# Warming products of 64 columns with none behind the last, and MLP weight roundings in halves in six of eight phases

## The chip, the core and the metric

The kernel runs on one core of a Trainium2 chip. The metric is the device time of one execution in microseconds (us); less is better. A second time, the span, is read from a profiled execution: it goes from the program's first to its last instruction.

## The reference

One transformer block on 512 rows of width 1024, in float32. A gated linear attention and a latent attention are merged, projected and added to the input `h`; then comes the MLP that the change touches:

```python
m = rmsnorm(h, g_mlp[l])
h = h + jnp.square(jax.nn.relu(m @ w_ff1[l])) @ w_ff2[l]
return rmsnorm(h, g_final)
```

`w_ff1` is 1024 x 4096, `w_ff2` 4096 x 1024. The first product of the whole program is a projection of the normed input on columns of `w_in`.

## The kernel before, in words

**Precision.** Each float32 operand is split in two fp32r tiles: a rounded part, whose name ends in `h` (ScalarE, ACT, rounds it by `activation(..., AF.Copy)`), and the remainder, whose name ends in `l` (VectorE, DVE, subtracts the rounded part from the source). A product is three matmuls on TensorE (PE): high by high, high by low, low by high (`mm3`, line 128).

**Start.** The first operands come by DMA. While they travel, PE multiplies a constant by itself into a bank that nobody reads (`warm`, lines 370 to 373): seven products of 128 columns and one of 64. In the profile each of these float32 products stands as two PE instructions, two passes, so `warm x16` is eight products. After them come the products called `first` (`first_by_sides`, line 450), in pieces of 256 columns, as the ACT and DVE roundings of their operands get done. This part is held in program order on each engine (`in_program_order(fixed)`, line 540).

**MLP.** The hidden width is done in four quarters (`NQ = 4`). Each quarter has two phases, `f` (`m @ w_ff1`) and `g` (the squared result `@ w_ff2`); the eight phases are `Mlp(0)` to `Mlp(7)`, called f0, g0, f1, g1, f2, g2, f3, g3, and `self.n` is the number. Each phase forms its 2 x 2 block product by seven block products (a scheme of the Strassen kind), called m = 1 to 7. For each m the weights stand in two groups `g` of 128 x 1024 elements; `hi(m, g)` (line 1725) rounds one into a tile such as `g031h` (phase g0, m = 3, group 1) and `lo(m, g)` (line 1737) makes the remainder `g031l` on DVE. A group is two pieces `p` of 128 x 512, which PE takes one after the other: in an f phase as the stationary operand, in a g phase as the moving one. The rounded tiles have four buffers of each kind (`halves`, line 251), so a rounding waits until PE has done with the product two before. In phases 2 and 4 (f1 and f2) a rounding is two ACT instructions of 128 x 512; in the other six it is one of 128 x 1024.

ACT does other work in between: copies of the f results out of their banks, relu, square, and the rounding of the squared rows (`left_hi`). DVE makes the remainders, adds the g results to the rows `h` (`add_rows`) and forms sums of blocks. Which step stands where is written by hand: tables of times (`PLACES`, `F0_PLACES`) sort the steps, and the order so made is kept on every engine (`in_program_order(written)`, line 2181).

**End.** `last_rows` (line 1878) finishes the last block product, norms the rows and stores them. The last product that counts goes into the bank `gend`. Behind it stand twelve products of 64 columns of `ones_r` into a bank `tail` (lines 1912 to 1914), which nobody reads. The order of the last steps is the string `LAST_ROWS` (`P:` is PE, `A:` ACT, `D:` DVE, `G:` GpSimd, `S:` the DMA queue of SyncE).

Of the kernel before, what the change touches and what calls it, by code (L numbers as in the profile page):

```python
# [18 lines left out]
P = 128  # L19
S = 512  # L20
NT = S // P
D = 1024
# [75 lines left out]
def tile_block(ctx: ExitStack, tc: tile.TileContext, t, out: bass.AP):  # L98
    nc = Held(tc.nc)
# [9 lines left out]
    def u2(name, dt=F32, shape=(P, S)):  # L109
        return tl(list(shape), dt, "u2", 29, name)  # L110

    def u4(name, dt=F32R, shape=(P, 2, S)):
        return tl(list(shape), dt, "u4", 26, name)
# [4 lines left out]
    def ps(tag, name):  # L118
        serial[0] += 1
        return pp.tile([P, S], F32, tag=tag, bufs=4, name=f"{name}_{serial[0]}")  # L120

    def one(shape, dt, name):
        return sb.tile(shape, dt, tag=name, bufs=1, name=name)
# [9 lines left out]
    def split(hi, lo, src, rest=nc.vector):  # L133
        nc.scalar.activation(hi, src, AF.Copy)
        rest.tensor_tensor(lo, src, raw(hi), op=ALU.subtract)
# [48 lines left out]
    ones_r = one([P, P], F32R, "ones_r")  # L184
# [66 lines left out]
    def halves(nk, nw, name):  # L251
        wh = tl([P, nk, nw], F32R, "wh", 4, f"{name}h")
        wl = tl([P, nk, nw], F32R, "wl", 4, f"{name}l")
        return wh, wl
# [114 lines left out]
    fixed = traced()  # L369
    warm = ps("at", "warm")  # L370
    heat = nc.const_aps.tensor(1.0, [P, P])
    for n in [P] * 7 + [P // 2]:
        nc.tensor.matmul(warm[:, :n], heat, heat[:, :n], start=True, stop=True)
    f_accs = [ps("mm", f"first{i}") for i in range(NT)]
    vh = [halves(2, S, f"first{k}") for k in range(KD // 2)]
    sq = None
# [1200 lines left out]
    def add_rows(i, c, acc, op=ALU.add):  # L1577
        hc = hrow[i][:, c * S : (c + 1) * S]
        nc.vector.tensor_tensor(hc, hc, acc, op=op)
# [115 lines left out]
    class Mlp:  # L1695
# [29 lines left out]
        def hi(self, m, g):  # L1725
            if (self.n, m) == (0, 1):
                self.right[m, g] = [u4(f"{self.name}{m}{g}{x}") for x in "hl"]
            else:
                self.right[m, g] = halves(2, S, f"{self.name}{m}{g}")
            src, to = self.tile_of(m)[g], self.right[m, g][0]  # L1730
            if self.n in (2, 4):
                for p in range(2):
                    nc.scalar.activation(to[:, p], src[:, p], AF.Copy)
            else:
                nc.scalar.activation(to, src, AF.Copy)
# [95 lines left out]
    def out_begin(i):  # L1831
        if not spare:
            spare.append(u2("junk"))
            nc.scalar.activation(ones_r, ident, AF.Copy)
            nc.scalar.activation(spare[0][:, 0:1], ident[:, 0:1], AF.Sqrt)
        hparts[i] = sm(f"hp{i}", 6)
        ms_rows[i] = u4(f"ms{i}", F32, (P, D))

    def out_square(i, src, n, at=0):
        nc.scalar.activation(  # L1840
            spare[0][:, at : at + src.shape[1]], src, AF.Square, accum_out=hparts[i][:, n : n + 1]
        )

    def out_mean(i):
        p = hparts[i]
        nc.gpsimd.tensor_scalar(p[:, 2:3], p[:, 0:1], 1.0 / D, EPS, op0=ALU.mult, op1=ALU.add)

    def out_added(i, n):
        p = hparts[i]
        nc.vector.scalar_tensor_tensor(  # L1850
            p[:, 2:3], p[:, n : n + 1], 1.0 / D, p[:, 2:3], op0=ALU.mult, op1=ALU.add
        )

    def out_rstd(i, n=1):
        p = hparts[i]
        nc.scalar.activation(p[:, 3:4], p[:, n : n + 1], AF.Sqrt, bias=p[:, 2:3], scale=1.0 / D)
        nc.vector.reciprocal(p[:, 5:6], p[:, 3:4])

    def out_gained(i, cols, eng=nc.gpsimd, src=None):
        src = hrow[i][:, cols] if src is None else src  # L1860
        eng.tensor_tensor(ms_rows[i][:, cols], src, gains[0][:, cols], op=ALU.mult)

    def out_scaled(i, cols, by_vector=False):
        o, rs = ms_rows[i][:, cols], hparts[i][:, 5:6]
        if by_vector:
            nc.vector.tensor_scalar(o, o, rs, None, op0=ALU.mult)
        else:
            nc.scalar.activation(o, o, AF.Copy, scale=rs)

    def out_left(i):  # L1870
        nc.vector.scalar_tensor_tensor(
            ms_rows[i][:, LEFT], hrow[i][:, LEFT], hparts[i][:, 5:6], gains[0][:, LEFT], op0=ALU.mult, op1=ALU.mult
        )

    def out_store(i, a, b, queue=nc.sync):
        queue.dma_start(out[0, i * P : (i + 1) * P, a:b], ms_rows[i][:, a:b])

    def last_rows(ph):

        accs, end = ph.acc_of[7], ps("mm", "gend")[:, 0:HT]  # L1880
        rest = u2("hend", F32R, (P, 2, HT))
        for i in (2, 3):
            out_begin(i)
            out_square(i, hrow[i][:, RIGHT], 0)
            out_mean(i)
            out_gained(i, RIGHT)
        split(rest[:, 0], rest[:, 1], hrow[3][:, QUARTERS[1]])
        nc.scalar.activation(end, accs[1][:, QUARTERS[1]], AF.Copy)
        for p in range(NP):
            ph.second_product(4, accs[0], False, 0, p)  # L1890
        for i in range(2):
            out_scaled(i, RIGHT)
            for a in (S, S + HT):
                out_store(i, a, a + HT)
            out_left(i)
            for a in (0, HT)[: 2 - i]:
                out_store(i, a, a + (HT, S)[i])
        add_rows(2, 0, accs[0])
        out_square(2, hrow[2][:, LEFT], 1)
        last = accs[1][:, QUARTERS[0]]  # L1900
        for p in range(NP):
            ph.second_product(4, last, False, 1, p, QUARTERS[0])
        out_rstd(2)
        nc.vector.tensor_tensor(hrow[3][:, QUARTERS[0]], last, hrow[3][:, QUARTERS[0]], op=ALU.add)
        out_square(3, hrow[3][:, QUARTERS[0]], 1)
        out_gained(3, QUARTERS[0], nc.vector)
        for p in range(NP):
            ph.second_product(4, end, False, 1, p, QUARTERS[1])
            if p == 2:
                for x in range(2):  # L1910
                    nc.tensor.matmul(end, ones_r, rest[:, x], start=False, stop=False, skip_group_check=True)
        tail = ps("mm", "tail")
        for _ in range(12):
            nc.tensor.matmul(tail[:, : P // 2], ones_r, ones_r[:, : P // 2], start=True, stop=True)
        out_scaled(2, RIGHT)
        out_store(2, S, D)
        out_left(2)
        out_store(2, 0, S)
        out_added(3, 1)
        out_square(3, end, 4, HT)  # L1920
        out_gained(3, QUARTERS[1], nc.vector, end)
        out_rstd(3, 4)
        cut = S + HT // 2
        out_scaled(3, slice(0, cut), True)
        out_scaled(3, slice(cut, D))
        out_store(3, 0, cut)
        out_store(3, cut, D, nc.scalar)
# [93 lines left out]
    for x in range(2):  # L2021
# [67 lines left out]
        P:g3x0*3 A:junk D:f3l41 G:hp0 A:hp0 P:g3x0*3 A:junk D:g340l P:g3x0*3 A:junk P:g3x1*3 D:f3l40 G:hp1 D:hp0  # L2089
        P:g3x0*3 A:hp1 A:g341h G:ms1 D:h2 D:hp1 A:ms0 S:out*2 P:g3x1*3 A:junk P:g3x1*3 D:g341l G:hp2 G:ms2 P:g3x1*3 A:gend D:ms0 S:out*2  # L2090
        A:ms1 S:out*2 D:h3 G:ms3 A:junk P:g3x0*12 D:ms1 S:out G:hp3 D:h2 D:hend A:junk
        P:g3x1*12 A:hp2 D:hp2 A:ms2 S:out D:h3 A:junk D:ms2 S:out D:ms3 D:hp3 P:gend*14 P:tail*12 A:junk D:ms3 A:hp3 D:hp3 D:ms3
        A:ms3 S:out A:out
    """
    FIRST, SECOND, PERIOD = 36, 22.77, 7857
# [81 lines left out]
    for _, _, what, args in [x for x in steps if x[0] >= last]:  # L2177
        what(*args)
    last_rows(g3)
    nc.emit(LAST_ROWS)  # L2180
    in_program_order(written)


def build(arrays):
    nc = bacc.Bacc("TRN2", target_bir_lowering=False, num_devices=1, dynamic_dma_scratch_size=8192)  # L2185
    t = {
        n: nc.dram_tensor(f"in_{n}", list(a.shape), mybir.dt.from_np(a.dtype), kind="ExternalInput").ap()
        for n, a in arrays.items()
    }
    out = nc.dram_tensor("out_0", [1, S, D], F32, kind="ExternalOutput").ap()  # L2190
    with tile.TileContext(nc) as tc:
        tile_block(tc, t, out)
    return nc
# [21 lines left out]
```

## Time and profile before

| | before |
|---|---|
| time, median of 3 runs | 733.57 us (733.51 to 733.57) |
| time of the profiled execution | 733.74 us |
| its span | 732.0 us |
| PE busy | 726.9 us, 99% of the span |
| DVE busy | 621.4 us, 85% |
| ACT busy | 502.2 us, 69% |
| GpSimd (POOL) busy | 224.6 us, 31% |

A row of the timeline reads: start in us from the span's start, length in us, engine, line, operation, what is written <- what is read, shape, count, and in brackets the engine's idle time ahead of it with what ended it. `PEld` is the loading of weights into PE, which overlaps with its matmuls. Equal instructions that follow each other are one row. Lines 76 and 90 are those of a helper that issues every instruction, so the tiles' names tell the rows apart. Matmul ends are modelled and overlap the next start: the step from start to start is what counts. `L2185` and the like are the program's frame.

### The profile page before, as it was taken

Reading aid. Unit: us, or ns where it says so; the run is one execution under the profiler, and the core shown is the slowest. Engines: PE = TensorE matmul, PEld = TensorE weight load, DVE = VectorE, ACT = ScalarE, POOL = GpSimd, SP = SyncE. Lnnn points to the kernel's source line nnn. Section 1 sums busy time; section 2 is a strip of 40 time slices with the busy share of each in tenths; the row PEclk is TensorE's granted clock in tenths of the full one; section 3 lists DMA queues with packets and bytes.
Section 4 is the critical chain, followed back from the end, with each engine's and each line's share of the span. In section 5 each row is a group of like instructions: output and inputs, shape, how many; then the busy total and the mean of one; then the engine's idle time right before and its main releaser. Section 6 shows DMA issues by size and latency. Waiting matters only on the chain.

```text
span 732.0 us, 11458 instructions
## 1 busy us (share of the span) xinstructions
PE 726.9 (99%) x4174; PEld 641.4 (88%) x4174; DVE 621.4 (85%) x861; ACT 502.2 (69%) x853; POOL 224.6 (31%) x283
## 2 busy tenths in 40 slices
PE   9999999999999999999999999999999999999997
PEld 8888888888898888888888999889988998899986
DVE  7777788889988887789989789998699869987797
ACT  7657565595686864988867889545774477546966
POOL 0742020234843843225873512200111012100224
PEclk9999999999999999999999999999999999999999
DMA  9848693431222334657957899871988078815754
GB/s 303 287 130 197 198 193 94 72 58 45 58 59 59 73 62 96 194 157 187 242 102 194 205 201 203 188 218 54 244 181 205 9 225 202 205 59 138 179 90 142
DMA packets 81625, 109.96 MB, mean 150 GB/s; under 512 B 16256, under 2 KB 35584, under 8 KB 81568
## 3 DMA queue, kind: packets, MB, share of 16 engines
q1 hardware_dynamic: 64192, 75.71, 33.3%
q0 software_dynamic: 17088, 33.30, 27.2%
q8 instruction: 33, 0.54, 0.3%
q10 hardware_dynamic: 288, 0.22, 0.1%
q14 instruction: 24, 0.20, 0.1%
HBM read 104.22 MB, written 2.10 MB: 145 GB/s over the span
## 4 chain that ended last, share of the span: by engine, by line
PE 97%; ACT 1%; POOL 1%; issue 1%; DVE 0%; POOLq 0%; ACTq 0%
PE first L90 3%; PE f3x L90 3%; PE f2x L90 3%; PE f1x L90 3%; PE f0x L90 3%; PE s L76 3%; PE av L76 3%; PE wox L76 3%; PE g2x L90 3%; PE g1x L90 3%; PE g0x L90 3%; PE gvx L90 3%; PE zax L90 3%; PE grx L90 3%; PE gk L90 2%; PE cq L90 2%
## 5 line engine op out<-in xcount | busy, mean ns | idle before, releaser
L90 POOL DMA_DIRECT2D w<-in_w_ff x32 | 38.6, 1205 | 240.1 <-DMA w<-in_w_ff 129.3
L76 ACT ACTIVATE e<-s,top 128x512 f32<-128x512 f32 x32 | 21.9, 687 | 8.1 <-DVE top L76 7.1
L76 PE MATMUL s<-kbuf,q 96*128 96x512 f32 x96 | 26.6, 403 | 0.0
L76 DVE TENSOR_REDUCE top<-s 128x1 f32<-128x512 f32 x32 | 21.6, 684 | 5.7 <-PE s L76 5.4
L76 PE MATMUL av<-pT,v 128*128 128x512 f32 (+1 forms) x108 | 25.4, 372 | 0.0
L76 DVE TENSOR_TENSOR pT<-tp,pT 128x512 fp32r<-128x512 f32 x32 | 21.7, 685 | 2.2 <-PE s L76 0.9
L76 ACT ACTIVATE pT<-tp 128x512 fp32r<-128x512 f32 x32 | 18.6, 600 | 5.8 <-PE tp L76 5.5
L76 PEld LDWEIGHTS av<-pT,v 128*128 128x128 f32 x108 | 18.6, 189 | 3.3
L76 PEld LDWEIGHTS s<-kbuf,q 96*128 96x128 f32 x96 | 17.0, 189 | 3.1 <-DVE grb L76 0.2
L76 PE MATMUL tp<-ident,e 128*128 128x128 f32 x128 | 17.9, 272 | 0.0
L76 PEld LDWEIGHTS tp<-ident,e 128*128 128x128 f32 x128 | 15.2, 140 | 2.7 <-ACT e L76 0.3
L90 POOL DMA_DIRECT2D gvw<-in_w_in x4 | 4.8, 1226 | 38.7 <-DVE gvw L90 34.0
L90 POOL TENSOR_TENSOR qF<-qk,qF 128x512 fp32r<-128x512 f32 x3 | 5.3, 1757 | 32.8 <-ACT qF L90 32.8
L90 POOL DMA_DIRECT2D zaw<-in_w_in x4 | 4.8, 1218 | 33.0 <-DVE zaw L90 28.3
L76 POOL DMA_DIRECT2D w<-in_w_ff x8 | 10.0, 1358 | 15.1 <-DVE g360l L76 7.1
L90 DVE TENSOR_TENSOR w<-w,w 128x1024 f32<-128x1024 f32 x12 | 14.4, 1222 | 0.1
L90 ACT ACT_TABLE_LOAD x9 | 11.5, 1283 | 1.2 <-PEq L2185 0.8
L76 POOL DMA_DIRECT2D w<-in_w_out x10 | 12.2, 1445 | 0.0
L76 POOL TENSOR_TENSOR my<-tb,yg 128x256 f32<-128x256 f32 x8 | 7.2, 899 | 13.7 <-DVE tb L76 7.5
L76 ACT ACTIVATE e<-e,tot 128x512 f32<-128x512 f32 x16 | 11.3, 721 | 0.0
L90 ACT ACTIVATE f1h<-f1a 128x512 fp32r<-128x512 f32 x10 | 6.1, 623 | 6.2 <-DVE f1a L90 6.2
L90 ACT ACTIVATE f0h<-f0a 128x512 fp32r<-128x512 f32 x10 | 6.1, 623 | 6.2 <-DVE f0a L90 6.2
(1979 smaller groups left out, 3106.0 us busy)
## 6 DMA issues: line engine op xcount, KB each, us to landing
w<-in_w_ff SPq DMA_DIRECT2D x48, 512.0 KB, 5.9
w<-in_w_ff POOLq DMA_DIRECT2D x40, 512.0 KB, 6.3
w<-in_w_out POOLq DMA_DIRECT2D x10, 512.0 KB, 6.1
grw<-in_w_in SPq DMA_DIRECT2D x8, 512.0 KB, 9.9
zaw<-in_w_in SPq DMA_DIRECT2D x8, 512.0 KB, 6.2
gvw<-in_w_in SPq DMA_DIRECT2D x8, 512.0 KB, 4.5
w<-in_w_out SPq DMA_DIRECT2D x16, 256.0 KB, 4.2
w221f<-in_w_ff SPq DMA_DIRECT2D x8, 512.0 KB, 5.0
```

The lines of the kernel that those rows point to most:

```text
L76: what(*args, **options)
L90: return what(*args, **options)
```

## The change

It has three edits.

1. The warming products become fifteen of 64 columns: 960 columns, as before (7 x 128 + 64), in 30 passes where there were 16.
2. The twelve `tail` products, and their bank, go.
3. `hi` rounds in two halves of 128 x 512 in all phases but f0 and g3: f1 and f2 did so already; g0, g1, g2 and f3 are new. That is 4 phases x 14 roundings = 56 more ACT instructions.

```diff
-    for n in [P] * 7 + [P // 2]:
-        nc.tensor.matmul(warm[:, :n], heat, heat[:, :n], start=True, stop=True)
+    for _ in range(15):
+        nc.tensor.matmul(warm[:, : P // 2], heat, heat[:, : P // 2], start=True, stop=True)
...
             src, to = self.tile_of(m)[g], self.right[m, g][0]
-            if self.n in (2, 4):
+            if 0 < self.n < 7:
                 for p in range(2):
                     nc.scalar.activation(to[:, p], src[:, p], AF.Copy)
             else:
...
-        tail = ps("mm", "tail")
-        for _ in range(12):
-            nc.tensor.matmul(tail[:, : P // 2], ones_r, ones_r[:, : P // 2], start=True, stop=True)
...
-P:gend*14 P:tail*12 A:junk
+P:gend*14 A:junk
```

No instruction of another kind moves: on DVE, GpSimd and SyncE the rows stand as before. The numbers in the names below are serials, which the added instructions shift.

PE's first rows before; `warm` is the bank that nobody reads, `first` are the accumulators of the first projection:

```order
L90 MATMUL warm_121<-const-float32-1.0 128x128 x7
L90 MATMUL warm_121<-const-float32-1.0 128x64
L90 MATMUL first_25_130<-xT_1_82,first0h_134 128x256
L90 MATMUL first_26_131<-xT_1_82,first0h_134 128x256
L90 MATMUL first_25_130<-xT_1_82,first0l_135 128x256
```

The same place now:

```order
L90 MATMUL warm_121<-const-float32-1.0 128x64 x15
L90 MATMUL first_25_137<-xT_1_82,first0h_141 128x256
L90 MATMUL first_26_138<-xT_1_82,first0h_141 128x256
L90 MATMUL first_25_137<-xT_1_82,first0l_142 128x256
L90 MATMUL first_26_138<-xT_1_82,first0l_142 128x256
```

Only the shape and the count of the warming rows differ; the first product keeps its place behind them.

ACT at the opening of phase g0 before; `g020h` to `g051h` are weight roundings, `f0a` relu and square of the rows of f0, `f0h` their roundings, `f0s` sums of blocks:

```order
L90 ACTIVATE g020h_4990<-w_30_802_2855 128x1024
L90 ACTIVATE f0a_977_4756<-f0a_977_4756 128x512
L90 ACTIVATE g021h_5009<-w_31_803_2856 128x1024
L90 ACTIVATE f0a_978_4757<-f0a_978_4757 128x512
L90 ACTIVATE f0h_1013_5021<-f0a_977_4756 128x512
L90 ACTIVATE f0a_978_4757<-f0a_978_4757 128x512
L90 ACTIVATE f0h_1014_5022<-f0a_978_4757 128x512
L90 ACTIVATE f0a_970_4686<-f0a_970_4686 128x512
L90 ACTIVATE f0h_1017_5042<-f0s_1001_4968 128x512
L90 ACTIVATE g050h_5051<-w_20_734_2787 128x1024
```

The same place now:

```order
L90 ACTIVATE g020h_4999<-w_30_802_2862 128x512 x2
L90 ACTIVATE f0a_977_4763<-f0a_977_4763 128x512
L90 ACTIVATE g021h_5019<-w_31_803_2863 128x512 x2
L90 ACTIVATE f0a_978_4764<-f0a_978_4764 128x512
L90 ACTIVATE f0h_1013_5032<-f0a_977_4763 128x512
L90 ACTIVATE f0a_978_4764<-f0a_978_4764 128x512
L90 ACTIVATE f0h_1014_5033<-f0a_978_4764 128x512
L90 ACTIVATE f0a_970_4693<-f0a_970_4693 128x512
L90 ACTIVATE f0h_1017_5053<-f0s_1001_4977 128x512
L90 ACTIVATE g050h_5062<-w_20_734_2794 128x512 x2
```

Each rounding is two rows' worth in the place of one; what stands between them stays where it was.

PE's last rows before; `gend` is the bank of the last product, `g341h` and `g341l` the last weights, `f3h` and `f3l` the squared rows, `hend` a part of the rows that is added on PE:

```order
L76 MATMUL gend_7526<-hend_7527,ones_r 128x256 x2
L76 MATMUL gend_7526<-g341h_7519,f3h_1322_7336 128x256
L76 MATMUL gend_7526<-g341l_7520,f3h_1322_7336 128x256
L76 MATMUL gend_7526<-g341h_7519,f3l_1324_7338 128x256
L76 MATMUL tail_7532<-ones_r 128x64 x12
L2191 UNCONDITIONAL_BRANCH
```

The same place now:

```order
L76 MATMUL gend_7589<-hend_7590,ones_r 128x256 x2
L76 MATMUL gend_7589<-g341h_7582,f3h_1322_7399 128x256
L76 MATMUL gend_7589<-g341l_7583,f3h_1322_7399 128x256
L76 MATMUL gend_7589<-g341h_7582,f3l_1324_7401 128x256
L2188 UNCONDITIONAL_BRANCH
```

The `tail` row is gone, and nothing takes its place.

More of the change, by code (lines that the diff above doesn't have):

```diff
@@ L2091, in tile_block @@
         A:ms1 S:out*2 D:h3 G:ms3 A:junk P:g3x0*12 D:ms1 S:out G:hp3 D:h2 D:hend A:junk
-        P:g3x1*12 A:hp2 D:hp2 A:ms2 S:out D:h3 A:junk D:ms2 S:out D:ms3 D:hp3 P:gend*14 P:tail*12 A:junk D:ms3 A:hp3 D:hp3 D:ms3
+        P:g3x1*12 A:hp2 D:hp2 A:ms2 S:out D:h3 A:junk D:ms2 S:out D:ms3 D:hp3 P:gend*14 A:junk D:ms3 A:hp3 D:hp3 D:ms3
         A:ms3 S:out A:out
```

## Prediction

> **What bounds the kernel now.** I read the page first, for the share of each engine and the chain that ended last:
>
> ```profile
> span 732.0 us, 11458 instructions
> ...
> PE 726.9 (99%) x4174; PEld 641.4 (88%) x4174; DVE 621.4 (85%) x861; ACT 502.2 (69%) x853; POOL 224.6 (31%) x283
> ...
> PE 97%; ACT 1%; POOL 1%; issue 1%; DVE 0%; POOLq 0%; ACTq 0%
> ```
>
> PE is busy for 726.9 of 732.0 us and is 97% of the chain. A busy PE may still step slowly, so next I asked the waits of PE alone. The whole answer is one row, the wait for the program's start:
>
> ```profile
> PE warm L90 <- PEq L2185: 0.8, 1, 0.8
> ```
>
> Then the busy times by stage: the phases f1, f2, f3 (the first three rows), g1 and g2. Columns: from:to, length, then busy time and count of PE, PEld, DVE, ACT, POOL, the granted clock, the DMA share and rate.
>
> ```profile
> 490.81:531.13 40.32, 40.32 (x338) 40.32 (x337) 31.01 (x32) 26.23 (x46) 3.73 (x4) 1.00 0.51 137
> 569.23:609.55 40.32, 40.32 (x338) 40.32 (x337) 31.01 (x32) 26.25 (x46) 3.76 (x4) 1.00 0.51 137
> 647.65:687.97 40.32, 40.32 (x338) 40.32 (x337) 31.04 (x32) 25.25 (x35) 3.73 (x4) 1.00 0.46 112
> 531.13:569.23 38.10, 38.10 (x170) 31.54 (x170) 36.46 (x48) 22.67 (x33) 5.90 (x5) 1.00 0.81 187
> 609.55:647.65 38.10, 38.10 (x170) 31.53 (x170) 36.45 (x48) 22.50 (x30) 5.90 (x5) 1.00 0.79 187
> ```
>
> An f phase has 336 products of 256 columns (the other two of the 338 began before), so a step is 40.32 / 336 = 0.120 us, and it is the same in all three. PE runs at its own pace through the MLP: nothing that makes weights ready earlier can shorten it, only something that makes them late can lengthen it. What is left to move lies before the first full-speed product and behind the last one.
>
> **Edit 1, the warming.** The start, by the timeline of PE, and then the rows of the `warm` and `tail` tiles' passes (count, shortest, median and longest in ns; nobody waits for `tail`), the timeline's row of `tail`, ACT's first rounding and a stage of PE alone (from:to, length, busy, count, clock, DMA):
>
> ```profile
> 0.84 3.65 PE L90 MATMUL warm<-const-float32-1.0 128*128 128x128 f32 x16 [0.84 <-PEq L2185]
> ...
> 3.75 0.53 PE L90 MATMUL warm<-const-float32-1.0 128*128 128x128 f32 x2
> ...
> 3.75 0.74 PE L90 MATMUL warm<-const-float32-1.0 128*128 128x128 f32 x3
> 4.28 0.80 PE L90 MATMUL first<-xT,first0h 128*128 128x256 f32 x2
> 4.87 0.63 PE L90 MATMUL first<-xT,first0l 128*128 128x256 f32 x2
> ...
> 6.15 0.71 PE L90 MATMUL first<-xT,first0h 128*128 128x256 f32 x3
> ```
>
> ```profile
> L90 PE MATMUL warm<-const-float32-1.0 x16: 314/421/550, 0.8 to 4.1; 128*128 128x128 f32 x14, 128*128 128x64 f32 x2
> ...
> L76 PE MATMUL tail<-ones_r x12: 194/277/277, 726.3 to 727.4; 128*128 128x64 f32 x12
> ...
> who waited for it (us, times):
> ...
> 726.29 1.42 PE L76 MATMUL tail<-ones_r 128*128 128x64 f32 x12
> ...
> 3.71 0.51 ACT L90 ACTIVATE xT<-xw 128x256 fp32r<-128x256 f32 x1 [1.63 <-DMA xw<-in_first]
> ...
> 6.58:8.98 2.40, 2.40 (x22) 1.00 1.04 380
> ```
>
> First, two speeds. From 4.87 to 6.15 stand six `first` products (three rows of two), (6.15 - 4.87) / 6 = 0.213 us each; from 6.58 to 8.98 stand 20 of the same shape (22 less the two that began before), 0.120 us each. The clock opens at 6.58. A us by which the real products start later is work done at the slow step, so it costs 1 - 0.120 / 0.213 = 0.44 us at the end.
>
> Second, how long the new warming takes. Before it, 13 passes of 128 columns lie between 0.84 and 3.75: 0.224 each, which includes the start of the first. The two short passes: the row of two ends at 3.75 + 0.53 = 4.28 with the pass of 0.314, which so began at 3.97; the row of three ends at 4.49 with one of 0.421, which so began at 4.07. So a pass of 64 columns, with a full load of 128 x 128 weights of its own, took about 0.10 to 0.11 us at the slow clock, half of a long one. Bounds for a pass of 64: 0.104 from below (the rows of `tail`, 12 passes at the fast clock: (1.42 - 0.277) / 11, where 0.277 is the length of one), and 0.213 from above (as if the columns made no difference). I take 0.112, half of 0.224, since the one direct row lies there. Then 30 passes take 3.36 us where the old 16 ended at 4.07 + 0.11 = 4.18, or 3.34 after 0.84. With a start-up of 0.14 on top (13 x (0.224 - 0.213)) the new ones end between 4.20 and 4.34. The first product waits for ACT's rounding anyway, 3.71 + 0.51 = 4.22, and began at 4.28; an end at 4.34 would make that 4.35, so all but 0.07 is hidden. On the path: 0 to 0.07 x 0.44 = 0.03 us. I take 0.03. If the cover were gone too, 0.07.
>
> [...]
>
> **Edit 2, the tail.** The end, from the last product that counts:
>
> ```profile
> 726.17 0.28 PE L76 MATMUL gend<-g341h,f3l 128*128 128x256 f32 x1
> ...
> 726.79 0.36 ACT L76 ACTIVATE junk<-gend 128x256 f32<-128x256 f32 x1
> ...
> 727.86 0.62 ACT L76 ACTIVATE ms<-ms,hp 128x384 f32<-128x384 f32 x1 [0.29 <-DVE hp L76]
> 728.51 0.36 ACTq L76 DMA_DIRECT2D out<-ms  x1
> ```
>
> PE's `tail` ends at 726.29 + 1.42 = 727.71; ACT goes on to 728.48, its store is issued at 728.51, and the span lasts to 732.0. Nobody waits for `tail`, and it stands behind everything that counts, so its 1.42 us are off the path: 0. The bounds are 0 both ways but for what follows on ACT and DVE being slower or faster without PE at work beside them, of which these rows show nothing.
>
> **Edit 3, the halves.** What two halves cost against one whole, in the same step of f1 and of f3 (ACT's timeline):
>
> ```profile
> 485.38 1.16 ACT L90 ACTIVATE f110h<-w 128x512 fp32r<-128x512 f32 x2 [0.93 <-PE g0x L90]
> ...
> 640.89 1.06 ACT L90 ACTIVATE f310h<-w 128x1024 fp32r<-128x1024 f32 x1
> ```
>
> 1.16 against 1.06: 0.10 us more, 56 x 0.10 = 5.6 us of ACT in four phases, 1.4 us in each. ACT is idle for 40.32 - 25.25 = 15 us in f3 and 38.10 - 22.67 = 15 us in g1. The halves free the first half for PE some 0.4 us earlier, which is worth nothing, since PE waits for none. For f3 the answer stands in the table above: f1 and f2 are that very code with halves, and take the same 40.32 us. In the g phases no row shows halves, so I looked for the tightest place, g0's m = 3, which recurs in g1 and g2:
>
> ```profile
> 453.39 1.05 ACT L90 ACTIVATE g021h<-w 128x1024 fp32r<-128x1024 f32 x1
> ...
> 464.68 0.63 ACT L90 ACTIVATE f0h<-f0a 128x512 fp32r<-128x512 f32 x1 [4.54 <-DVE f0a L90]
> ```
>
> ```profile
> 454.54 1.22 DVE L90 TENSOR_TENSOR g021l<-w,g021h 128x1024 fp32r<-128x1024 f32 x1
> ...
> 468.71 1.22 DVE L90 TENSOR_TENSOR g031l<-w221f,g031h 128x1024 fp32r<-128x1024 f32 x1
> ...
> 449.86:476.96 27.10, 27.10 (x132) 22.91 (x131) 27.09 (x36) 19.01 (x28) 6.13 (x6) 1.00 0.90 196
> ...
> 470.25 0.19 PEld L90 LDWEIGHTS g0z<-g031l,f0h 128*128 128x128 f32 x1
> ```
>
> `g031l` is ready at 468.71 + 1.22 = 469.93, and PE comes for it at 470.25: a cover of 0.32 us, the smallest of the 42 in g0 to g2. DVE is busy for 27.09 of 27.10 us around it, so a delay that gets into DVE stays there. One does: `g021h` ends at 454.44 and `g021l` starts at 454.54, a slack of 0.10, while two halved roundings on ACT bring 0.20. DVE slips by about 0.1 to 0.13 and the cover shrinks to about 0.2. Later roundings do not add: ACT's backlog is cleared in its idle 4.54 us before 464.68, and from there DVE is later than ACT. So 0 on the path. If the cover did not hold, four roundings' 0.4 less 0.32 is 0.08 in each of three phases, 0.24.
>
> **The sum.** The profiled execution took 733.74 us with a span of 732.0; the median of the plain runs, 733.57, is 0.17 below it, and I count from there: 733.57 + 0.03 (warming) + 0 (tail) + 0 (halves) = 733.6 us. A measurement of this kernel can tell about 0.2% from no change, 1.47 us; this is far inside.
>
> **The rivals.**
>
> - *The clock opens late* (slower). The place is the clock's step at 6.58. If short passes do not count as work for whatever opens the clock, it opens later by the warming's 4.28 - 0.84 = 3.44 us, each worth 0.44: 1.5 us, 735.1. It decides as soon as the step to 0.120 comes after about 9.9. For it: the opening came 5.74 us after PE's first pass, so most of that time was warming. Against it: columns and weight loads per us are the same. [...] The trace shows one opening and can't tell more. Chance 0.05.
> - *Short passes cost as much as long ones.* 30 x 0.213 = 6.4 us; the clock opens on the way and the first product starts near 7.0, and the ten real passes that were begun by 6.58 follow in 10 x 0.120 = 1.2 us, to 8.2: 1.6 later, 735.2. Against it is the direct row of 0.10 to 0.11. Chance 0.02.
> - [...] Chance 0.03.
> - *ACT's backlog reaches PE*: up to 0.24, 733.8, as worked out; a chance of 0.03, of which 0.01 for much more.
> - *The change doesn't do what it says*: each edit leaves the columns, the stored rows and the products as they were, so this is the forecast itself. It has 0.87.
>
> **How the numbers follow.** Slower by over 0.2%: 0.05 + 0.02 + 0.01 = 0.08. Faster by over 0.2%: no case gives it; 0.01 for what I don't see. Within 0.2%: 0.91. The range takes the forecast with the clock's opening uncertain by 1 us either way (0.44), and above that the 0.24: 733.1 to 734.3.
>
> **What would show it.** Right: 30 `warm` passes about 0.11 apart, the first real product at 4.28 to 4.35, the step to 0.120 near 6.58, f3 at 40.32 and g1 and g2 at 38.10 us, PE waiting for nothing in them, and the last store some 2 us behind `gend`. Wrong: a step of 0.213 in the warming or after 6.6, a g phase over 38.2 us, or an end that moves against `gend`.

## The result, and the profile after

The changed kernel took 737.97 us (median of 6 runs, 737.02 to 738.79) against 733.55 us before (733.16 to 733.81): a ratio of 1.0060, 95% interval 1.0047 to 1.0073. It is slower by about 4.4 us, where 733.6 was forecast. The profiled execution took 737.02 us, with a span of 735.3 us:

```profile
span 735.3 us, 11520 instructions
...
PE 728.9 (99%) x4176; PEld 643.3 (87%) x4176; DVE 621.6 (85%) x861; ACT 507.4 (69%) x909; POOL 224.5 (31%) x283
```

PE is again busy for 99%. The span is longer by 3.3 us; the first place to look is PE's own start (timeline: the first row is the weight loads of the warming, the last one ACT's rounding that the first real product needs):

```profile
0.80 6.47 PEld L90 LDWEIGHTS warm<-const-float32-1.0 128*128 128x128 f32 x30 [0.80 <-issue]
...
0.83 6.63 PE L90 MATMUL warm<-const-float32-1.0 128*128 128x64 f32 x30 [0.83 <-PEq L2182]
7.23 0.77 PE L90 MATMUL first<-xT,first0h 128*128 128x256 f32 x2
7.80 0.63 PE L90 MATMUL first<-xT,first0l 128*128 128x256 f32 x2
8.22 0.63 PE L90 MATMUL first<-xT,first0h 128*128 128x256 f32 x2
8.65 0.63 PE L90 MATMUL first<-xT,first0l 128*128 128x256 f32 x2
9.08 2.07 PE L90 MATMUL first<-xT,first0h 128*128 128x256 f32 x12
...
3.68 0.51 ACT L90 ACTIVATE xT<-xw 128x256 fp32r<-128x256 f32 x1 [1.60 <-DMA xw<-in_first]
```

The 30 passes of 64 columns last 6.63 us: less the last one's length of 0.42, that is 6.21 / 29 = 0.214 us a step, the step that a pass of 128 columns had before, not half of it. The loads keep the same pace: less the last one's 0.33, (6.47 - 0.33) / 29 = 0.212. So the first real product starts at 7.23 where it started at 4.28, 2.95 us later, though its operand is rounded at 4.19. And the slow step goes on for longer: from 7.80 to 9.08 stand six products at 0.213. The row of twelve at 9.08 shows where it ends. At the slow step its length would be 11 x 0.213 + 0.42 = 2.76, at the fast one 11 x 0.120 + 0.28 = 1.60; it is 2.07, so five steps were slow, (2.07 - 1.60) / 0.093, and the fast step came within it, near 10.1. Before, it came at 6.58 with ten real products begun; now thirteen had been. Three more steps at 0.093 above the fast one are 0.28. With the 2.95 that is 3.23 of the span's 3.3.

The MLP, by stage (f1, f3, g1, g2; columns as in the prediction):

```profile
494.07:534.39 40.32, 40.32 (x338) 40.32 (x337) 31.01 (x32) 26.44 (x49) 3.73 (x4) 1.00 0.52 137
650.91:691.23 40.32, 40.32 (x338) 40.32 (x337) 31.01 (x32) 26.25 (x46) 3.73 (x4) 1.00 0.45 112
534.39:572.49 38.10, 38.10 (x170) 31.53 (x170) 36.59 (x48) 23.69 (x44) 5.90 (x5) 1.00 0.80 188
612.81:650.91 38.10, 38.10 (x170) 31.54 (x170) 36.51 (x48) 23.82 (x44) 5.90 (x5) 1.00 0.80 187
```

They last exactly as long as before, and each begins 3.26 us later (f1 490.81, now 494.07). ACT's busy time grows by about 1.0 to 1.3 us in each newly halved phase and nobody waits for it. The tight place of the prediction, by ACT's, DVE's and PEld's rows:

```profile
456.75 1.14 ACT L90 ACTIVATE g021h<-w 128x512 fp32r<-128x512 f32 x2
...
457.92 1.23 DVE L90 TENSOR_TENSOR g021l<-w,g021h 128x1024 fp32r<-128x1024 f32 x1
...
472.07 1.22 DVE L90 TENSOR_TENSOR g031l<-w221f,g031h 128x1024 fp32r<-128x1024 f32 x1
...
473.51 0.19 PEld L90 LDWEIGHTS g0z<-g031l,f0h 128*128 128x128 f32 x1
```

`g021h` now ends at 457.89 and `g021l` starts 0.03 later; `g031l` is ready at 473.29, 0.22 before PE comes, where it was 0.32. The end:

```profile
729.43 0.28 PE L76 MATMUL gend<-g341h,f3l 128*128 128x256 f32 x1
...
730.05 0.36 ACT L76 ACTIVATE junk<-gend 128x256 f32<-128x256 f32 x1
...
731.77 0.36 ACTq L76 DMA_DIRECT2D out<-ms  x1
```

From the last product to the last store lie 731.77 - 729.43 = 2.34 us, as before (728.51 - 726.17). Nearly all of the loss in this trace lies ahead of 10.99 us: the row that starts there started at 7.78 before, 3.21 earlier.

The profiled execution is the fastest of the six, whose spans go from 735.3 to 737.1 us. So this trace accounts for 3.3 us, and not for all of the 4.4 by which the medians differ; the slower executions have no trace. Two runs below, e8 and e5, give a measure: there the fast step comes 5.3 and 5.6 us after the first real product, here 2.9. A fast step as late as theirs would add about 1.1 to 1.2 us at 0.44 each, an estimate.

### The profile page after: what moved, and what is told of

The parts are those of the page before. It is cut to its first block, busy times and chain, and to the rows that moved or that the text cites. A ratio compares the mean times of both kernels' runs of the same rounds, so it can differ in the third digit from the quotient of the medians.

```text
span 735.3 us, 11520 instructions
## 1 busy us (share of the span) xinstructions
PE 728.9 (99%) x4176; PEld 643.3 (87%) x4176; DVE 621.6 (85%) x861; ACT 507.4 (69%) x909; POOL 224.5 (31%) x283
## 4 chain that ended last, share of the span: by engine, by line
PE 97%; ACT 1%; POOL 1%; issue 1%; DVE 0%; POOLq 0%; ACTq 0%
PE first L90 3%; PE f3x L90 3%; PE f2x L90 3%; PE f1x L90 3%; PE f0x L90 3%; PE s L76 3%; PE av L76 3%; PE wox L76 3%; PE g2x L90 3%; PE g1x L90 3%; PE g0x L90 3%; PE gvx L90 3%; PE zax L90 3%; PE grx L90 3%; PE gk L90 2%; PE cq L90 2%
## 5 line engine op out<-in xcount | busy, mean ns | idle before, releaser
L90 ACT ACTIVATE f2h<-f2a 128x512 fp32r<-128x512 f32 x10 | 6.2, 626 | 5.9 <-DVE f2a L90 5.9
L90 POOL TENSOR_TENSOR qk<-qkf,c3f 128x256 f32<-128x256 f32 x11 | 9.8, 919 | 0.2
```

Of the source, the lines that this page charges most:

```text
L90: return what(*args, **options)
```

## The experiments

Theory A, a guess from the load rows above and their pace of 0.212 us: a float32 pass can't step faster than its weights load, so the thirty short passes last 6.4 us. Theory B, a guess that goes with it: time in which a pass fills only half of its step doesn't bring the fast step, so that comes late as well. Filled is meant by columns: 64 of them took the step of 0.214 us that 128 took before, so a pass of 128 counts as filled and one of 64 as half filled. Rival C: the halves or the missing tail take part. Each run is set against the kernel before on the same chip, where that took 733.65 us (median of 27 executions) beside e1 to e4, 733.52 (27) beside e5 to e8 and 733.32 (15) beside e9 to e12.

"The slow clock" in the prediction and the expectations is the slow step, 0.213 us, and "the clock opens" is the change to the fast one, 0.111 to 0.120. The traces show the steps alone: the profile's own clock column reads 1.00 in the slow stretches too (e9's first stretch below). That a clock is behind the change is the author's reading and was not shown.

### One edit at a time

The warming alone:

```diff
-    for n in [P] * 7 + [P // 2]:
-        nc.tensor.matmul(warm[:, :n], heat, heat[:, :n], start=True, stop=True)
+    for _ in range(15):
+        nc.tensor.matmul(warm[:, : P // 2], heat, heat[:, : P // 2], start=True, stop=True)
```

> The kernel before with the fifteen warming products of 64 columns alone. Theory A (each short pass takes as long as one of 128 columns at the slow clock, 0.213 us, so the warming lasts 30 x 0.213 = 6.4 us and the first real product starts near 7.2, with the clock opening later as well): all of the change's loss, 738 us, 4 to 5 above before. Rival C (part of the loss comes from the halves or from the missing tail): well below 738, by that part.

Measured: 737.24 us, ratio 1.0049 (1.0036 to 1.0061). That is 3.6 us, against 4.4 for the whole change. The intervals overlap, so the difference can't be told from none.

The halves alone:

```diff
-            if self.n in (2, 4):
+            if 0 < self.n < 7:
```

> The kernel before with the roundings in halves in phases 1 to 6 alone. Theory A: no difference, 733.5 within 0.2 us, f and g phases at 40.32 and 38.10 us. Rival C: slower by up to 4 us.

Measured: 733.54 us, ratio 0.9999 (0.9990 to 1.0007). No difference in the time. But in its trace one phase did last longer: g1 took 38.44 us from its first product to the first of f2, not 38.10. ACT's rounding of `g141h`, and PE's load of its remainder:

```profile
562.41 1.15 ACT L90 ACTIVATE g141h<-w 128x512 fp32r<-128x512 f32 x2 [3.50 <-DMA w<-in_w_ff]
...
564.88 0.19 PEld L90 LDWEIGHTS g1x<-g141l,f1h 128*128 128x128 f32 x1 [0.44 <-DVE g141l L90]
```

The weights came late by DMA: ACT waited 3.50 us for them, 2.23 in the trace of before. The halves took 1.15 where the whole took 1.06 there, so at most about 0.1 of the 0.33 lost is theirs, an estimate. The changed kernel and e4, with the same halves, kept 38.10 in g1.

The tail alone:

```diff
-        tail = ps("mm", "tail")
-        for _ in range(12):
-            nc.tensor.matmul(tail[:, : P // 2], ones_r, ones_r[:, : P // 2], start=True, stop=True)
...
-P:gend*14 P:tail*12 A:junk
+P:gend*14 A:junk
```

> The kernel before without the twelve products behind the last, alone. Theory A: no difference, 733.5 within 0.2 us. Rival C (the tail does something for the end, or for the clock at the next start): slower, by up to 4 us.

Measured: 733.12 us, ratio 0.9994 (0.9985 to 1.0003): no difference that can be told. The trace has the finer answer, the last product and the last store:

```profile
725.29 0.28 PE L76 MATMUL gend<-g341h,f3l 128*128 128x256 f32 x1
...
727.62 0.35 ACTq L76 DMA_DIRECT2D out<-ms  x1
```

2.33 us between them, against 2.34 with the tail.

The changed kernel with the old warming:

```diff
-    for _ in range(15):
-        nc.tensor.matmul(warm[:, : P // 2], heat, heat[:, : P // 2], start=True, stop=True)
+    for n in [P] * 7 + [P // 2]:
+        nc.tensor.matmul(warm[:, :n], heat, heat[:, :n], start=True, stop=True)
```

> The changed kernel with the old warming put back (halves and no tail stay). Theory A: back to 733.5 within 0.2 us. Rival C: stays above by what the two other edits cost together.

Measured: 733.21 us, ratio 0.9997 (0.9988 to 1.0006). The loss is gone. So the halves and the missing tail don't bring it, alone or together, and rival C falls. This version is not clearly faster than the kernel before either.

### Length and filling, apart

Eight products of 64 columns: as many passes as before, half filled.

```diff
-    for n in [P] * 7 + [P // 2]:
+    for n in [P // 2] * 8:
```

> The kernel before with eight warming products of 64 columns: 16 passes, as before, with fewer columns. A pass takes 0.213 us whatever its columns (theory A), so the warming ends near 4.3 as before and the first real product starts at 4.28 to 4.35. Length alone: no difference, 733.6. Theory B (a pass of 64 columns fills only half of its 0.213 us, and half-filled time doesn't open the clock): the step to 0.120 comes later by up to 3.4 us, 734 to 735.2 us. If a pass of 64 took 0.107 us, the warming would end near 2.7 and PE would sit idle until 4.28.

Measured: 734.33 us, ratio 1.0013 (1.0004 to 1.0022). Its PE rows:

```profile
0.84 3.65 PE L90 MATMUL warm<-const-float32-1.0 128*128 128x64 f32 x16 [0.84 <-PEq L2185]
4.40 0.79 PE L90 MATMUL first<-xT,first0h 128*128 128x256 f32 x2
...
6.28 2.76 PE L90 MATMUL first<-xT,first0h 128*128 128x256 f32 x12
```

Sixteen short passes last as long as before's fourteen long ones and two short. The real products start on time, within 0.12 us, but the row of twelve is 2.76 long: slow to its end. Length is the same, the fast step is late, and that costs 0.8 us in the median. The trace shows the slowest of the 11 executions, 735.23 us.

Fifteen products of 128 columns: as many passes as in the change, filled.

```diff
-    for n in [P] * 7 + [P // 2]:
+    for n in [P] * 15:
```

> The kernel before with fifteen warming products of 128 columns: 30 passes, as many as in the changed kernel, each filled. Length alone: as the changed kernel, 737 to 738. Theory B: PE is as long in the warming, but filled, so the clock opens within it, before about 7.7; the rest of the warming and all real products run fast: 734.3 to 735.3, that is 1 to 2 us above before and 2 to 4 below the changed kernel.

Measured: 734.85 us, ratio 1.0019 (1.0011 to 1.0028).

```profile
0.84 5.82 PE L90 MATMUL warm<-const-float32-1.0 128*128 128x128 f32 x30 [0.84 <-PEq L2185]
6.42 0.48 PE L90 MATMUL first<-xT,first0h 128*128 128x256 f32 x2
...
7.45 1.60 PE L90 MATMUL first<-xT,first0h 128*128 128x256 f32 x12
```

Thirty filled passes are shorter than thirty half-filled ones, 5.82 against 6.63, because the fast step comes on the way; all real products run at the fast step (the row of twelve is 1.60). The length by itself costs 1.3 us. The two by themselves, 0.8 and 1.3, do not add up to the warming's 3.6: in the change, the first products that are not half filled begin only at 7.23, and the fast step came 2.9 us behind that, so the two delays build on each other.

The step by width, one execution:

```diff
-    for n in [P] * 7 + [P // 2]:
+    for n in [P // 4] * 2 + [P // 2] * 2 + [3 * P // 4] * 2 + [P] * 2:
```

> The kernel before with a warming of 2 products each of 32, 64, 96 and 128 columns, 16 passes, one look at their steps at the slow clock. Theory A (the load of the weights sets the step): 0.213 us for all four widths, the first real product at 4.28 to 4.35. Rival (the columns set it): 0.053, 0.107, 0.160 and 0.213 us, and PE idle from about 3.0 to 4.28.

Measured, in the row of the tile (shortest, median, longest ns) and the first rows of PE:

```profile
L90 PE MATMUL warm<-const-float32-1.0 x16: 391/421/474, 0.8 to 4.2; 128*128 128x32 f32 x4, 128*128 128x64 f32 x4, 128*128 128x96 f32 x4, 128*128 128x128 f32 x4
...
0.84 3.76 PE L90 MATMUL warm<-const-float32-1.0 128*128 128x32 f32 x16 [0.84 <-PEq L2185]
4.44 0.79 PE L90 MATMUL first<-xT,first0h 128*128 128x256 f32 x2
```

Sixteen passes, four of each width, in 3.76: (3.76 - 0.42) / 15 = 0.22 a step over all. By columns alone it would have been 0.053 to 0.213, 0.13 on average. Over these four widths the step does not fall with the columns, as theory A has it. The first real product starts at 4.44, a little later than the 4.28 to 4.35 expected. Every pass here carries a full load, so whether it is the load or something else of a float32 pass that takes 0.213 us was not taken apart; for the load speaks that the load rows keep this pace (0.212 in the changed kernel). The run took 733.75 us.

No warming. It leaves out only products whose result nobody reads.

```diff
-    heat = nc.const_aps.tensor(1.0, [P, P])
-    for n in [P] * 7 + [P // 2]:
-        nc.tensor.matmul(warm[:, :n], heat, heat[:, :n], start=True, stop=True)
```

> The kernel before with no warming products; it leaves out only work whose result nobody reads. The first real product starts at 4.28, with its operands, and the clock opens later by about what the warming lasted, 3.44 us, at 0.44 us each: 1.5 us, 735.1. If the changed kernel's 738 is above this, its warming is worse than none: that is the case under both theory A and theory B.

Measured: 735.13 us, ratio 1.0018 (1.0009 to 1.0028).

```profile
4.38 0.80 PE L90 MATMUL first<-xT,first0h 128*128 128x256 f32 x2 [4.38 <-ACT xT L90]
...
6.26 2.76 PE L90 MATMUL first<-xT,first0h 128*128 128x256 f32 x12
```

The old warming is worth 1.6 us, where 1.5 was expected from 0.44 us for each us of delay. The change's warming, at 1.0049 by itself (e1), is worse than none.

### What brings the fast step

Sixty-four half-filled passes, one execution:

```diff
-    for n in [P] * 7 + [P // 2]:
+    for n in [P // 2] * 32:
```

> The kernel before with 32 warming products of 64 columns: 64 passes of 0.213 us, half filled, one look. Theory B (half-filled passes don't open the clock, however long they go on): the step stays 0.213 us through the whole warming, to 0.84 + 64 x 0.213 = 14.5 us, and the clock opens 2 to 6 us after the first real product. [...]

Measured: 744.01 us. PE's rows, and two stages of PE alone (from:to, length, busy, count, clock, DMA):

```profile
0.84 13.89 PE L90 MATMUL warm<-const-float32-1.0 128*128 128x64 f32 x64 [0.84 <-PEq L2185]
14.48 0.77 PE L90 MATMUL first<-xT,first0h 128*128 128x256 f32 x2
...
14.50:16.80 2.30, 2.30 (x13) 1.00 1.22 291
16.92:18.92 2.00, 2.00 (x19) 1.00 1.09 354
```

(13.89 - 0.42) / 63 = 0.214 through the whole warming: in 13.9 us with PE never idle the fast step did not come. It came about 2.4 us after filled products began: 10 in 2.30 (13 less three begun before) are 0.23 a step up to 16.8, the long first one among them, and 17 in 2.00 (19 less two) are 0.118 from 16.92.

Sixty-four passes of 96 columns, one execution:

```diff
-    for n in [P] * 7 + [P // 2]:
+    for n in [3 * P // 4] * 32:
```

> The kernel before with 32 warming products of 96 columns: 64 passes of 0.213 us, three quarters filled, one look. It places the bound between half and full: if the step falls from 0.213 to about 0.11 within the warming (before 7.7), three quarters are enough; if it stays at 0.213 to 14.5 us, they are not. [...]

Measured: 739.23 us.

```profile
0.84 9.99 PE L90 MATMUL warm<-const-float32-1.0 128*128 128x96 f32 x64 [0.84 <-PEq L2185]
...
1.00:6.30 5.30, 5.30 (x26) 1.00 0.83 233
6.40:10.50 4.10, 4.10 (x39) 1.00 1.04 387
```

24 or 25 steps in 5.30 are 0.21 to 0.22; then 37 in 4.10 are 0.111. With passes three quarters filled the fast step came before 6.4, within 5.6 us of the first of them; with passes half filled it did not come in 13.9 us (e9). That is one execution each.

Operands of two bytes, one execution:

```diff
-    for n in [P] * 7 + [P // 2]:
-        nc.tensor.matmul(warm[:, :n], heat, heat[:, :n], start=True, stop=True)
+    narrow = nc.const_aps.tensor(1.0, [P, P], mybir.dt.bfloat16)
+    for n in [P // 2] * 12:
+        nc.tensor.matmul(warm[:, :n], narrow, narrow[:, :n], start=True, stop=True)
+    for n in [P] * 5:
+        nc.tensor.matmul(warm[:, :n], heat, heat[:, :n], start=True, stop=True)
```

> The kernel before with a warming of twelve bf16 products of 64 columns (one pass each) and five float32 ones of 128 (ten passes), one look at the step of a pass whose weights are two bytes wide. [...]

Measured: 732.86 us, one run; the lowest of the 15 executions of before is 732.94.

```profile
0.81 0.67 PEld L90 LDWEIGHTS <-const-bfloat16-1.0 128*128 128x128 bf16 x12 [0.81 <-issue]
...
0.84 0.80 PE L90 MATMUL warm<-const-bfloat16-1.0 128*128 128x64 bf16 x12 [0.84 <-PEq L2188]
1.45 2.48 PE L90 MATMUL warm<-const-float32-1.0 128*128 128x128 f32 x10
4.24 0.51 PE L90 MATMUL first<-xT,first0h 128*128 128x256 f32 x2 [0.31 <-ACT xT L90]
```

A bf16 pass of 64 columns steps by (0.80 - 0.24) / 11 = 0.05 us, with a load of 128 x 128 of its own: a quarter of the 0.213 of a float32 one. The fast step had not come yet: the ten float32 passes behind take (2.48 - 0.42) / 9 = 0.23 each. So a load of 128 columns did not take 0.213 us here, with bf16; that step is measured with float32 alone. Weights and moving operand are both bf16 here, so which of the two lifts it was not taken apart.

Sixteen passes of 32 columns:

```diff
-    for n in [P] * 7 + [P // 2]:
+    for n in [P // 4] * 8:
```

> The kernel before with eight warming products of 32 columns: 16 passes of 0.213 us, a quarter filled. The first real product at 4.28 to 4.4 as before. Theory B: worth no more than no warming at all, 735.1, against 734.3 with 64 columns and 733.5 before. Rival (the loads of the weights count as work for the clock): 733.5.

Measured: 734.85 us, ratio 1.0015 (1.0006 to 1.0024), its PE rows:

```profile
0.84 3.59 PE L90 MATMUL warm<-const-float32-1.0 128*128 128x32 f32 x16 [0.84 <-PEq L2185]
4.26 0.79 PE L90 MATMUL first<-xT,first0h 128*128 128x256 f32 x2
...
6.14 2.76 PE L90 MATMUL first<-xT,first0h 128*128 128x256 f32 x12
```

On time, and slow through the row of twelve. By its interval it can't be told from no warming (1.0018) or from passes of 64 (1.0013). It agrees with theory B and excludes the rival, in which the loads alone count; it does not rank 32 against 64.

## Why the prediction was wrong

**What bounds the kernel** was right: PE steps at its own pace through the MLP, and f3, g1 and g2 kept 40.32 and 38.10 us.

**The tail** was right at 0: the last store stands 2.34 us behind the last product with and without it.

**The halves** were right at 0, with their mechanism: two halves took 1.14 to 1.16 where the whole took 1.05, DVE's remainder slipped at `g021l`, and the cover at `g031l` went from 0.32 to 0.22, where about 0.2 was forecast. What it did not have is e2's late DMA, which reached PE at `g141l` and made g1 longer than its sign of 38.2.

**The warming** failed, at the step "So a pass of 64 columns, with a full load of 128 x 128 weights of its own, took about 0.10 to 0.11 us at the slow clock, half of a long one." The reading took one interval between two recorded starts for a pace. There was just one such pair in the trace, nothing of its own kind came behind it, and the next product was 0.21 later. The load rows of the same trace, of the kernel before, show the pace:

```profile
3.54 0.76 PEld L90 LDWEIGHTS warm<-const-float32-1.0 128*128 128x128 f32 x3
...
3.75 0.55 PEld L90 LDWEIGHTS warm<-const-float32-1.0 128*128 128x128 f32 x2
...
3.96 0.33 PEld L90 LDWEIGHTS warm<-const-float32-1.0 128*128 128x128 f32 x1
...
3.96 0.53 PE L90 MATMUL warm<-const-float32-1.0 128*128 128x64 f32 x2
...
4.07 0.42 PE L90 MATMUL warm<-const-float32-1.0 128*128 128x64 f32 x1
```

The last three loads start at 3.54, 3.75 and 3.96, 0.21 apart, for short passes as for long ones. The pass at 3.96, behind one of 128 columns, starts 0.21 after its load (3.75); the pass at 4.07, behind one of 64, 0.10 after its load (3.96). That lag shrinks once, where the width changes, and so two starts lie 0.107 apart. It is no pace. Where others of its width follow, a pass of 32 columns steps by 0.213 us ((3.59 - 0.40) / 15, e12), one of 64 by 0.214 (e9), one of 96 by 0.21 to 0.22 (e10), and the loads for 128 by 0.21 (above). The term was 0.03 us; the warming alone measured 3.6 (1.0049, e1) and the whole change 4.4. Two of the prediction's own signs of being wrong came: a step of 0.213 in the warming, and after 6.6.

**The two rivals that came true** were kept apart. "Short passes cost as much as long ones" had 735.2, on the premise that the fast step comes on the way, at 6.58; that is the case of filled passes, and e6 measured it at 1.3 us above before. "The clock opens late" had 735.1, on the premise that the first product starts at 4.28; e5 and e8 measured that at 0.8 and 1.6. The price of the one changes when the other holds, and by theories A and B, which the runs fit and do not prove, both follow from one cause: a pass that waits for its weights is long and half empty. The 0.44 for a us of delay holds while the fast step comes at a fixed time; in the change it moved with the start, from 6.58 to about 10.1, and the 2.95 us of delay cost 2.95. "Columns and weight loads per us are the same" was the argument against the late one. By the prediction's own pace the loads per us would have nearly doubled (30 in 3.36 us where 16 took 3.34), and with the measured pace the columns per us were half.

**The range** left out a bound that the prediction itself had named. It said 0.213 from above for the pass, priced that at 735.2, and ended at 734.3.

**An early fast step**, with a chance of 0.03, was the author's estimate, and no run shows it as a gain: in e3, with the old warming, the fast step stands from 4.81 on, where before's came at 6.58 (last section), and its median, 733.12 us, can't be told from before's.

## What to carry to other kernels

Count a warming in filled time, not in instructions or in columns. Here a float32 pass with weights of its own took 0.21 to 0.22 us at the slow step at each width tried, 32 to 128 columns; 13.9 us of passes of 64 brought no fast step (e9), and thirty passes of 128 brought it within their 5.82 us (e6). So fill them. Read a pace from three or more equal instructions in a row, never from one interval, and compare it with the load rows. When a bound from above is only argued away, keep it in the range. Where two rivals share a cause, price them together.

## What the runs showed of the hardware that was not expected

- Float32 passes of 32, 64, 96 and 128 columns, each with a load of 128 x 128 weights, stepped by 0.21 to 0.22 us at the start (e7, e9, e10, e12), and those of 96 columns by 0.111 later (e10); bf16 passes of 64 columns stepped by 0.05, ahead of float32 ones at 0.23 (e11).
- A PE that was busy without a gap for 13.9 us kept the slow step with its passes half filled (0.214, e9), and left it before 6.4 us with three quarters (e10), one execution each.
- After a warming of passes filled to one half or a quarter, the fast step came 2.4 to 5.6 us after the first real product (the changed kernel, e1, e5, e9, e12); with no warming 5.3 us (e8); with the old warming 0.6 and 2.3 us (e3, before).
- The moment of the fast step differed between two executions with the same warming and nearly the same start (4.28 and 4.25). It was 6.58 in the profile of before; in that of e3, the real products were at the fast step from 4.81 on, and the row of twelve lasts 1.60:

```profile
4.25 0.73 PE L90 MATMUL first<-xT,first0h 128*128 128x256 f32 x2
4.81 0.41 PE L90 MATMUL first<-xT,first0l 128*128 128x256 f32 x2
...
5.53 1.60 PE L90 MATMUL first<-xT,first0h 128*128 128x256 f32 x12
```

The same row of before:

```profile
6.15 1.79 PE L90 MATMUL first<-xT,first0h 128*128 128x256 f32 x12
```

At its end e3 is 0.8 us ahead (7.13 against 7.94), which is nearly all of the 0.9 by which its profiled span, 731.1 us, is shorter; the missing tail has no part in that. Spreads like that of before beside e1 to e4, 732.87 to 734.45 us over 27 executions, fit with it; that they come from that moment alone was not tested.
